# The order in which the moving operand's columns are read in seven input projections of a hybrid decoder layer

## The chip, the cores and the metric

The kernel runs on one core of one Trainium2 chip. The metric is the device time of one execution in microseconds (us); lower is better. Of the kernel before, two executions were timed, 2161.64 and 2170.17 us, with a median of 2165.9 us.

## What is computed

One decoder layer over 512 tokens of width 2048, in float32. One input projection is split by columns between gated linear attention (GLA, 4 heads) and differential softmax attention (4 heads). Their outputs pass through one output projection, and a gated MLP with a short causal convolution follows. The part that matters here is the first line of the token mixer:

```
proj = h @ w_in
offs = np.cumsum((0,) + IN_SPLITS)
gq, gk, gv, gg, ga, dq, dk, dv = [proj[..., int(offs[i]):int(offs[i + 1])]
                                  for i in range(len(IN_SPLITS))]
...
o_a = gla_chunked(gq..., gk..., gv..., log_a...)
o_b = diff_attention(dq..., dk..., dv, lam)
o = concatenate([rmsnorm(o_a) * gate, rmsnorm(o_b) * (1.0 - lambda_init)])
return o @ w_o
```

`h` is the normalised input (512 x 2048). The columns of `w_in` are 512 for gq, 512 for gk, 1024 for gv, 1024 for gg, 16 for ga, and 1024 each for dq, dk and dv.

## The kernel before, in words

**Number format.** Every large matrix product is done on numbers split in two. `ah` and `al` hold the high and low halves of the transposed activations, each as a tile of 128 partitions by (4 token groups, 16 slices of the model width, 128 tokens) of 4-byte fp32r numbers. A weight block of 128 x 1024 is loaded by one DMA (`load`, L100), and `granule` (L126) splits it: ScalarE copies the high half into the buffer `ring` (L135) and VectorE subtracts it to get the low half (L136). `ring` has three slots of a high and a low half. A product is then three matmuls, high by high, high by low, and low by high, all added into one PSUM bank of 128 x 512.

**Two forms of projection.** `proj_t` (L176) gives two 128-column pieces of the output with the tokens along the columns of the bank. The weight is the stationary operand, and the moving operand is `ah[:, t0:t1, kk, :]` or the same slice of `al`: four runs of 128 tokens. From one run to the next it is 16 x 128 elements of 4 bytes, 8192 bytes, and within a run the step is 4 bytes. One call has 4 granules, and each granule has 2 pieces x 4 slices x 3 = 24 matmuls, so it is 96 matmuls of 512 columns. `proj_n` (L194) gives 512 output columns for each of the four token groups, in four banks. Here `ah` and `al` are stationary and the weight is the moving operand: one run of 512 elements. One call has 8 granules of 4 token groups x 2 slices x 3 = 24 matmuls, so it is 192 matmuls of 512 columns. In both, the matmul writes its bank column by column in sequence.

**Evictions.** When a projection is complete, `emit` is called once per bank: two times in `proj_t`, four times in `proj_n`. For gq, gk, gv, dq, dk and dv it is one ScalarE copy of 128 x 512 from the bank to an SBUF tile (L311, L569, L571, L577, L583, L585). The gate (gg) has another form (L588).

**Order of the work.** After a first part whose order is written by hand (`first_half`, L219), the projections run in program order: gq and gk of heads 0 and 1, the second half of gv, gq and gk of heads 2 and 3, the first half of dv, dq and dk of differential head 0, of head 1, the second half of dv, dq and dk of heads 2 and 3, and then gg. After each granule, `step` (L84) takes one or two pieces from a list of small jobs (`fill`): forget gate, GLA heads, differential heads. Their small matmuls are thus placed between the projection's matmuls on TensorE's queue. A planner that estimates times sets the final order on each engine. The projections take their banks from a pool of four (`psm`), and the fill jobs from another pool of four. After the mixer come the output projection (L637 to L739) and the MLP, which together take most of the time and use the same `proj_t`, `mm_t`, `proj_n` and `mm_n` for a part of it.

Of the kernel before, what the change touches and what calls it, by code (L numbers as in the profile page):

```python
# [12 lines left out]
AF = mybir.ActivationFunctionType  # L13
# [4 lines left out]
P = 128  # L18
D = 2048
S = 512  # L20
NT = S // P
KT = D // P
EPS = 1e-6
GH, GDK, GDV, RANK = 4, 128, 256, 16
# [5 lines left out]
C_GQ, C_GK, C_GV, C_GG, C_GA, C_DQ, C_DK, C_DV = 0, 512, 1024, 2048, 3072, 3088, 4112, 5136  # L30
# [5 lines left out]
def hybrid_layer(ctx: ExitStack, tc: tile.TileContext, x, attn_pre_norm, w_in, w_alpha_up, b_alpha,  # L36
# [5 lines left out]
    w_in3 = w_in[0].rearrange("(k p) c -> p k c", p=P)  # L42
# [9 lines left out]
    act = nc.scalar.activation  # L52
# [3 lines left out]
    mm = nc.tensor.matmul  # L56
# [16 lines left out]
    ah = const.tile([P, NT, KT, P], F32R, name="ah")  # L73
    al = const.tile([P, NT, KT, P], F32R, name="al")
    wpool = ctx.enter_context(tc.tile_pool(name="w", bufs=3))

    def bank(pool=None):
        return (pool or psa).tile([P, 512], F32, name="bank", tag="bank")
# [5 lines left out]
    def step(n=None):  # L84
        pace[1] += pace[0]
        while pace[1] >= 1.0:
            pace[1] -= 1.0
            while fill:
                try:
                    next(fill[0])  # L90
                    break
                except StopIteration:
                    fill.pop(0)
# [6 lines left out]
    def load(src, a):  # L100
        raw = wpool.tile([P, GR], F32, name="raw", tag="raw", bufs=4)
        dma(raw.rearrange("p (a b) -> p a b", a=a), src)
        return raw
# [7 lines left out]
    def halves():  # L111
        slot[0] = (slot[0] + 1) % 3
        return [ring[:, GR * i + place_w[0]:GR * (i + 1) + place_w[0]] for i in (slot[0], slot[0] + 3)]
# [3 lines left out]
    def spare_halves(pool):  # L117
        if pool == "rt":
            return [rp.tile([P, GR], F32R, name=n, tag="rt", bufs=4) for n in ("xhi", "xlo")]
        if pool is True:  # L120
            if not kept:
                kept.extend(small_tile(n, F32R) for n in ("xhi", "xlo"))
            return kept
        return [pool.tile([P, GR], F32R, name=n, tag=n, bufs=4) for n in ("xhi", "xlo")]

    def granule(src, a, raw=None, spare=None, hl=None):  # L126
        if raw is None:
            raw = load(src, a)
        if hl is not None:
            hi, lo = hl[:, 0, :], hl[:, 1, :]  # L130
        elif spare:
            hi, lo = spare_halves(spare)
        else:
            hi, lo = halves()
        act(hi, raw, AF.Copy)  # L135
        tt(lo, raw, hi.bitcast(F32), ALU.subtract)  # L136
        r = "p (a b) -> p a b"
        return hi.rearrange(r, a=a), lo.rearrange(r, a=a)
# [21 lines left out]
    def bcast_row(tile_ap, row):  # L160
        dma(tile_ap, row.partition_broadcast(P))

    def mm_t(banks, g, w, t0, t1):
        for n in range(2):
            for k in range(4):
                kk = 4 * g + k
                wh = w[0][:, k, n * P:(n + 1) * P]
                wl = w[1][:, k, n * P:(n + 1) * P]
                o = banks[n][:, t0 * P:t1 * P].rearrange("p (t c) -> p t c", c=P)
                st, sp = kk == 0, kk == KT - 1  # L170
                mm(o, wh, ah[:, t0:t1, kk, :], start=st, stop=False)  # L171
                mm(o, wh, al[:, t0:t1, kk, :], start=False, stop=False)  # L172
                mm(o, wl, ah[:, t0:t1, kk, :], start=False, stop=sp)  # L173


    def proj_t(w3, col, emit):  # L176
        banks = [bank(psm) for _ in range(2)]
        for g in range(KT // 4):
            mm_t(banks, g, granule(w3[:, 4 * g:4 * g + 4, col:col + 256], 4), 0, NT)
            if g == KT // 4 - 1:  # L180
                for n in range(2):
                    emit(n, banks[n])
            step()

    def mm_n(banks, t, g, w):
        for k in range(2):
            s = 2 * g + k
            st, sp = s == 0, s == KT - 1
            mm(banks[t], ah[:, t, s, :], w[0][:, k, :], start=st, stop=False)  # L189
            mm(banks[t], ah[:, t, s, :], w[1][:, k, :], start=False, stop=False)  # L190
            mm(banks[t], al[:, t, s, :], w[0][:, k, :], start=False, stop=sp)  # L191


    def proj_n(w3, col, emit, order=tuple(range(KT)), first=0, banks=None):  # L194
        if banks is None:
            banks = [bank(psm) for _ in range(NT)]
        for g in range(first, KT // 2):
            w = granule(w3[:, order[2 * g]:order[2 * g] + 2, col:col + 512], 2)
            for t in range(NT):
                mm_n(banks, t, g, w)  # L200
                if g == KT // 2 - 1:
                    emit(t, banks[t])
            step()

    mixer = ExitStack()
# [3 lines left out]
    def big8(name):  # L209
        return mx.tile([P, 2048], F32, name=name, tag="big8", bufs=6)  # L210

    def qk_tile(name):
        return mx.tile([P, S], F32, name=name, tag="qk", bufs=6)
# [5 lines left out]
    def first_half(c):  # L219
# [37 lines left out]
        def prods(t, *gs):  # L257
            for g in gs:
                mm_n(banks, t, g, w[g])
# [46 lines left out]
    with tc.manual_schedule(engines=IN_ORDER):  # L306
        banks = first_half(0)
    gv = [big8("gv").rearrange("p (t e) -> p t e", t=NT) for _ in range(2)]

    def gv_out(c):  # L310
        return lambda t, b: act(gv[c][:, t, :], b, AF.Copy)  # L311

    proj_n(w_in3, C_GV, gv_out(0), first=4, banks=banks)


# [250 lines left out]

    def gla_qk(hp):
        q = [qk_tile("gq") for _ in range(2)]
        proj_t(w_in3, C_GQ + 256 * hp, lambda n, b: act(q[n], b, AF.Copy, scale=GDK ** -0.5))  # L569
        k = [qk_tile("gk") for _ in range(2)]  # L570
        proj_t(w_in3, C_GK + 256 * hp, lambda n, b: act(k[n], b, AF.Copy))  # L571
        for i in range(2):
            fill.append(gla_head(2 * hp + i, q[i], k[i]))

    def diff_v(g):
        dv = big8("dv").rearrange("p (t e) -> p t e", t=NT)
        proj_n(w_in3, C_DV + 512 * g, lambda t, b: act(dv[:, t, :], b, AF.Copy))  # L577
        dst = big8("dst").rearrange("p (j s) -> p j s", j=4)
        return dv, dst

    def diff_qk(h, dv, dst):
        q = [qk_tile("dq") for _ in range(2)]
        proj_t(w_in3, C_DQ + 256 * h, lambda n, b: act(q[n], b, AF.Copy))  # L583
        k = [qk_tile("dk") for _ in range(2)]
        proj_t(w_in3, C_DK + 256 * h, lambda n, b: act(k[n], b, AF.Copy))  # L585
        fill.append(diff_head(h, q, k, dv, dst))

    def gate(c, t, b):  # L588
# [4 lines left out]

    fill.append(forget_gate())
    gla_qk(0)
    pace[0] = 1.7
    proj_n(w_in3, C_GV + 512, gv_out(1))
    gla_qk(1)
    dsts = []
    for g in range(2):  # L600
        dv, dst = diff_v(g)
        dsts.append(dst)
        diff_qk(2 * g, dv, dst)
        pace[0] = 1.0
        diff_qk(2 * g + 1, dv, dst)
# [3 lines left out]
    for g in range(2):  # L609
        for j in range(4):  # L610
            s = 4 * g + j
# [29 lines left out]
    def to_ffn():  # L641
# [6 lines left out]
        def prods(t, *gs):  # L648
            for g in gs:
                mm_n(banks, t, g, w[g])  # L650
# [60 lines left out]
        ba = [bank(psm) for _ in range(2)]  # L711
        bb = [bank(psm) for _ in range(2)]
        mm_t(ba, 0, wa[0], 0, 2)
        residual(3)
        turn(2, 0, 1, 2, 3)
        square(3)
        weights_f(wa, 0, 3, wp)
        mm_t(ba, 1, wa[1], 0, 2)
        mm_t(ba, 2, wa[2], 0, 2)
        scale(3)  # L720
# [364 lines left out]
    for i, u in enumerate(downs):  # L1085
        nxt = downs[i + 1] if i + 1 < len(downs) else None
        nc_ = (i + 1) // 2
        first = i % 2 == 0
# [23 lines left out]
        else:  # L1112
            for j in range(2):
                for half, c, op in ((1, 0, ALU.add), (1, 1, ALU.subtract), (0, 1, ALU.subtract)):
                    dst = acc[2 * half + j].rearrange("p (b c x) -> p b c x", b=2, c=2)[:, :, c, :]
# [125 lines left out]
```

## Time and profile before

| | |
|---|---|
| timed executions | 2161.64 and 2170.17 us, median 2165.9 us |
| span of the profiled execution, first to last instruction | 2150.8 us |
| time of the profiled execution itself | not given beside its span; the median is 15.1 us above the span |
| TensorE busy (PE) | 2112.4 us, 98% of the span |
| TensorE weight loads (PEld) | 1875.4 us, 87% |
| VectorE busy (DVE) | 1414.6 us, 66% |
| ScalarE busy (ACT) | 898.3 us, 42% |
| DMA | 303.83 MB, mean 141 GB/s |

How to read it: the busy time of TensorE is the union of its matmuls, each of which lasts from its start to its modelled end. Matmuls are pipelined, so one starts before the one ahead of it has ended. What a matmul costs the engine is therefore the distance from its start to the next one's start, which the timeline gives, and not its duration in the list of groups. In the list of groups, a row is: line, engine, operation, the tile written and the tiles read, the shape, the count, then the busy time in us, the mean duration of one in ns, and the idle time of the engine before it.

### The profile page before, as it was taken

How to read it: one execution, taken by the hardware profiler on the slowest of the kernel's cores; microseconds unless marked ns; L12 is line 12 of the kernel's file. 1: busy time of each engine (PE TensorE's matmuls, PEld its weight loads, DVE VectorE, ACT ScalarE, POOL GpSimd, SP SyncE). 2: the span in 40 equal slices, each digit the busy share in tenths (PEclk: the TensorE clock that was granted, in tenths of full speed). 3: DMA queues.
4: the chain of work that ended last, by engine and by line, in shares of the span. 5: the costliest groups of instructions: out<-in, count | busy, mean ns of one | idle time of the engine just before them, and what ended most of it. 6: DMA issues, size and time to landing. Idle time of an engine off the chain costs nothing.

```text
span 2150.8 us, 31861 instructions
## 1 busy us (share of the span) xinstructions
PE 2112.4 (98%) x13009; PEld 1875.4 (87%) x13009; DVE 1414.6 (66%) x1725; ACT 898.3 (42%) x1162; POOL 199.2 (9%) x242
## 2 busy tenths in 40 slices
PE   7999999999999999999999999999999899999998
PEld 6878888888888889999999999999999778787786
DVE  5345554443444237688777786777778777888887
ACT  4233332333343224344544553544454554443433
POOL 1000000000000001011111111111110111110100
PEclk9999999999999999999999999999999999999999
DMA  6322222223224335455776757667577777676653
GB/s 214 99 75 79 79 69 79 79 79 88 78 80 169 95 128 186 128 119 136 172 172 149 175 139 189 149 157 191 129 172 177 203 229 182 171 195 170 158 167 145
DMA packets 218471, 303.83 MB, mean 141 GB/s; under 512 B 11776, under 2 KB 155572, under 8 KB 216404
## 3 DMA queue, kind: packets, MB, share of 16 engines
q1 hardware_dynamic: 165204, 238.87, 33.4%
q0 software_dynamic: 53120, 62.92, 19.1%
q8 instruction: 102, 1.67, 0.3%
q14 instruction: 45, 0.37, 0.1%
HBM read 273.97 MB, written 27.79 MB: 140 GB/s over the span
## 4 chain that ended last, share of the span: by engine, by line
PE 46%; issue 45%; POOL 4%; DVE 3%; DMA 2%; ACT 1%; POOLq 0%; SPq 0%; DVEq 0%; ACTq 0%
PE bank L189 7%; PE bank L190 7%; PE bank L191 7%; PE bank L173 5%; PE bank L171 5%; PE bank L172 5%; POOL rt L873 2%; PE bank L926 2%; PE bank L925 2%; PE bank L924 2%; POOL raw L873 2%; PE bank L439 1%; PE bank L507 1%; PE bank L538 1%; DVE ring L136 1%
## 5 line engine op out<-in xcount | busy, mean ns | idle before, releaser
L136 DVE TENSOR_TENSOR ring<-raw,ring 128x1024 fp32r<-128x1024 f32 x305 | 371.6, 1221 | 353.8 <-ACT ring L135 344.1
L135 ACT ACTIVATE ring<-raw 128x1024 fp32r<-128x1024 f32 x305 | 323.1, 1060 | 596.6 <-PE bank L191 157.3
L926 PE MATMUL bank<-ah,ring 128*128 128x256 f32 x1280 | 353.7, 276 | 0.8 <-DVE ring L136 0.8
L924 PE MATMUL bank<-ah,ring 128*128 128x256 f32 x1280 | 353.5, 276 | 0.0
L925 PE MATMUL bank<-al,ring 128*128 128x256 f32 x1280 | 353.4, 276 | 0.0
L136 DVE TENSOR_TENSOR ring<-rt,ring 128x1024 fp32r<-128x1024 f32 x221 | 269.0, 1220 | 89.8 <-ACT ring L135 87.9
L135 ACT ACTIVATE ring<-rt 128x1024 fp32r<-128x1024 f32 x221 | 233.1, 1060 | 223.5 <-PE bank L925 146.1
L926 PEld LDWEIGHTS bank<-ah,ring 128*128 128x128 f32 x1280 | 240.3, 188 | 1.2 <-DVE ring L136 1.2
L925 PEld LDWEIGHTS bank<-al,ring 128*128 128x128 f32 x1280 | 240.4, 188 | 0.1
L924 PEld LDWEIGHTS bank<-ah,ring 128*128 128x128 f32 x1280 | 240.3, 188 | 0.1
L189 PE MATMUL bank<-ring,ah 128*128 128x512 f32 x600 | 236.9, 398 | 0.8 <-ACT ah L148 0.8
L190 PE MATMUL bank<-ring,ah 128*128 128x512 f32 x600 | 235.8, 394 | 0.0
L191 PE MATMUL bank<-ring,al 128*128 128x512 f32 x600 | 235.0, 394 | 0.0
L171 PE MATMUL bank<-ah,ring 128*128 128x512 f32 (+1 forms) x512 | 196.2, 383 | 0.0
L173 PE MATMUL bank<-ah,ring 128*128 128x512 f32 (+1 forms) x512 | 194.7, 380 | 0.0
L172 PE MATMUL bank<-al,ring 128*128 128x512 f32 (+1 forms) x512 | 194.5, 380 | 0.0
L1022 PE MATMUL bank<-ring,ah 128*128 128x512 f32 x424 | 166.7, 393 | 7.3 <-DVE ring L136 7.2
L1023 PE MATMUL bank<-ring,al 128*128 128x512 f32 x424 | 165.8, 391 | 0.0
L1021 PE MATMUL bank<-ring,ah 128*128 128x512 f32 x424 | 158.8, 393 | 3.2 <-ACT ring L135 2.4
L191 PEld LDWEIGHTS bank<-ring,al 128*128 128x128 f32 x600 | 113.2, 189 | 24.3 <-DVE al L149 0.3
L189 PEld LDWEIGHTS bank<-ring,ah 128*128 128x128 f32 x600 | 113.1, 189 | 24.2 <-ACT ah L148 1.2
L190 PEld LDWEIGHTS bank<-ring,ah 128*128 128x128 f32 x600 | 113.3, 189 | 23.7 <-DVE ring L136 0.5
(260 smaller groups left out, 4063.6 us busy)
## 6 DMA issues: line engine op xcount, KB each, us to landing
raw<-in_w_in_dram SPq DMA_DIRECT2D x96, 512.0 KB, 3.7
raw<-in_w_ffn_in_dram SPq DMA_DIRECT2D x96, 512.0 KB, 5.1
raw<-in_w_ffn_out_dram SPq DMA_DIRECT2D x48, 512.0 KB, 7.3
rt<-in_w_ffn_in_dram SPq DMA_DIRECT2D x40, 512.0 KB, 6.6
rt<-in_w_ffn_in_dram POOLq DMA_DIRECT2D x40, 512.0 KB, 6.2
raw<-in_w_ffn_in_dram POOLq DMA_DIRECT2D x40, 512.0 KB, 6.8
raw<-in_w_o_dram SPq DMA_DIRECT2D x32, 512.0 KB, 3.7
rt<-in_w_ffn_out_dram SPq DMA_DIRECT2D x20, 512.0 KB, 8.1
```

The source lines that it names most:

```text
L135: act(hi, raw, AF.Copy)
L136: tt(lo, raw, hi.bitcast(F32), ALU.subtract)
L171: mm(o, wh, ah[:, t0:t1, kk, :], start=st, stop=False)
L172: mm(o, wh, al[:, t0:t1, kk, :], start=False, stop=False)
L173: mm(o, wl, ah[:, t0:t1, kk, :], start=False, stop=sp)
L189: mm(banks[t], ah[:, t, s, :], w[0][:, k, :], start=st, stop=False)
L190: mm(banks[t], ah[:, t, s, :], w[1][:, k, :], start=False, stop=False)
L191: mm(banks[t], al[:, t, s, :], w[0][:, k, :], start=False, stop=sp)
L924: mm(o, wh, sh[:, :, kk, :], start=start and kk == 0 and n == 0, stop=False, **NOW)
L925: mm(o, wh, sl[:, :, kk, :], start=False, stop=False, **NOW)
L926: mm(o, wl, sh[:, :, kk, :], start=False, stop=kk == HK - 1, **NOW)
L1022: mm(b[j], sh[:, o:o + P], w[1][:, q, :], start=False, stop=False, **NOW)
```

## The change

Seven of the input projections read the columns of the moving operand in another order. Bank columns are still written in sequence, so the result lies in the bank in the walked order, and the eviction writes its destination in that order, which puts every column back in its place. Two counters give each call of `proj_t` and of `proj_n` on `w_in` its walk; the calls after the list's end, the first call of `proj_n`, the first call of `proj_t`, and all calls on other weights keep the order of before.

The walks by projection, with `c` a column within a token group and `t` the token group:

| name here | projection | order of the moving operand's columns |
|---|---|---|
| T1 | gk, heads 0 and 1 | the four token groups innermost: each column lies 8192 bytes from the one before, and after four of them the next is 4 bytes further on |
| T2 | gq, heads 2 and 3 | in each token group every second column, then the others: step 8 bytes |
| T3 | gk, heads 2 and 3 | runs of 64 neighbouring columns, going through the token groups |
| T4 | dq, head 0 | runs of 16 neighbouring columns, going through the token groups |
| N1 | gv, second half | every sixteenth column: step 64 bytes |
| N2 | dv, first half | every second column, then the others: step 8 bytes |
| N3 | dv, second half | runs of 16 neighbouring columns, taken in turn from the two halves |

The core of the diff:

```diff
-    def mm_t(banks, g, w, t0, t1):
+    WALKS = {"t": [("p t c -> p t c", {}), ("p t c -> p c t", {}), ("p t (c b) -> p t b c", dict(b=2)),
+                   ("p t (b c) -> p b t c", dict(b=2)), ("p t (b c) -> p b t c", dict(b=8))],
+             "n": [("p c -> p c", {}), ("p (a b) -> p b a", dict(a=32)), ("p (b a) -> p a b", dict(a=2)),
+                   ("p (a b c) -> p b a c", dict(a=2, c=16))]}
+    calls = {"t": 0, "n": 0}
+
+    def next_walk(kind):
+        i = calls[kind]
+        calls[kind] += 1
+        return i if i < len(WALKS[kind]) else 0
+
+    def walk(kind, i, ap):
+        how, sizes = WALKS[kind][i]
+        return ap.rearrange(how, **sizes)
+
+    def as_walked(kind, i, b, like):
+        names = WALKS[kind][i][0].split("-> p ")[1]
+        dims = dict(zip(names.split(), walk(kind, i, like).shape[1:]))
+        first = names.split()[0]
+        dims.pop(first)
+        return b.rearrange(f"p ({names}) -> p {names}", **dims)
+
+    def mm_t(banks, g, w, t0, t1, i=0):
...
-                mm(o, wh, ah[:, t0:t1, kk, :], start=st, stop=False)
-                mm(o, wh, al[:, t0:t1, kk, :], start=False, stop=False)
-                mm(o, wl, ah[:, t0:t1, kk, :], start=False, stop=sp)
+                xh, xl = (walk("t", i, v[:, t0:t1, kk, :]) for v in (ah, al))
+                if i:
+                    o = as_walked("t", i, banks[n], ah[:, t0:t1, kk, :])
+                mm(o, wh, xh, start=st, stop=False)
+                mm(o, wh, xl, start=False, stop=False)
+                mm(o, wl, xh, start=False, stop=sp)
...
     def proj_t(w3, col, emit):
         banks = [bank(psm) for _ in range(2)]
+        i = next_walk("t") if w3 is w_in3 else 0
...
-    def mm_n(banks, t, g, w):
+    def mm_n(banks, t, g, w, i=0):
...
-            mm(banks[t], ah[:, t, s, :], w[0][:, k, :], start=st, stop=False)
-            mm(banks[t], ah[:, t, s, :], w[1][:, k, :], start=False, stop=False)
-            mm(banks[t], al[:, t, s, :], w[0][:, k, :], start=False, stop=sp)
+            wh, wl = (walk("n", i, v[:, k, :]) for v in w)
+            o = as_walked("n", i, banks[t], w[0][:, k, :]) if i else banks[t]
+            mm(o, ah[:, t, s, :], wh, start=st, stop=False)
+            mm(o, ah[:, t, s, :], wl, start=False, stop=False)
+            mm(o, al[:, t, s, :], wh, start=False, stop=sp)
...
+    def put_n(dst, b, i):
+        act(walk("n", i, dst), as_walked("n", i, b, dst), AF.Copy)
+
+    def put_t(dst, b, i, **kw):
+        d = dst.rearrange("p (t c) -> p t c", c=P)
+        act(walk("t", i, d), as_walked("t", i, b, d), AF.Copy, **kw)
+
     def gv_out(c):
-        return lambda t, b: act(gv[c][:, t, :], b, AF.Copy)
+        return lambda t, b, i=0: put_n(gv[c][:, t, :], b, i)
...
-        proj_t(w_in3, C_GK + 256 * hp, lambda n, b: act(k[n], b, AF.Copy))
+        proj_t(w_in3, C_GK + 256 * hp, lambda n, b, i=0: put_t(k[n], b, i))
```

The evictions of gq, dv, dq and dk are changed in the same way as that of gk.

More of the change, by code (lines that the diff above doesn't have):

```diff
@@ L170, in mm_t @@
                 st, sp = kk == 0, kk == KT - 1
-                mm(o, wh, ah[:, t0:t1, kk, :], start=st, stop=False)
-                mm(o, wh, al[:, t0:t1, kk, :], start=False, stop=False)
-                mm(o, wl, ah[:, t0:t1, kk, :], start=False, stop=sp)
+                xh, xl = (walk("t", i, v[:, t0:t1, kk, :]) for v in (ah, al))
[4 more added lines that the diff above has]
+                mm(o, wl, xh, start=False, stop=sp)
     def proj_t(w3, col, emit):
         banks = [bank(psm) for _ in range(2)]
+        i = next_walk("t") if w3 is w_in3 else 0
         for g in range(KT // 4):
-            mm_t(banks, g, granule(w3[:, 4 * g:4 * g + 4, col:col + 256], 4), 0, NT)
+            mm_t(banks, g, granule(w3[:, 4 * g:4 * g + 4, col:col + 256], 4), 0, NT, i)
             if g == KT // 4 - 1:
                 for n in range(2):
-                    emit(n, banks[n])
+                    if i:
+                        emit(n, banks[n], i)
+                    else:
+                        emit(n, banks[n])
             step()
-    def mm_n(banks, t, g, w):
+    def mm_n(banks, t, g, w, i=0):
         for k in range(2):
@@ L196, in proj_n @@
             banks = [bank(psm) for _ in range(NT)]
+        i = next_walk("n") if w3 is w_in3 else 0
         for g in range(first, KT // 2):
@@ L199, in proj_n @@
             for t in range(NT):
-                mm_n(banks, t, g, w)
+                mm_n(banks, t, g, w, i)
                 if g == KT // 2 - 1:
-                    emit(t, banks[t])
+                    if i:
+                        emit(t, banks[t], i)
+                    else:
+                        emit(t, banks[t])
             step()
@@ L568, in gla_qk @@
         q = [qk_tile("gq") for _ in range(2)]
-        proj_t(w_in3, C_GQ + 256 * hp, lambda n, b: act(q[n], b, AF.Copy, scale=GDK ** -0.5))
+        proj_t(w_in3, C_GQ + 256 * hp, lambda n, b, i=0: put_t(q[n], b, i, scale=GDK ** -0.5))
         k = [qk_tile("gk") for _ in range(2)]
-        proj_t(w_in3, C_GK + 256 * hp, lambda n, b: act(k[n], b, AF.Copy))
+        proj_t(w_in3, C_GK + 256 * hp, lambda n, b, i=0: put_t(k[n], b, i))
         for i in range(2):
@@ L576, in diff_v @@
         dv = big8("dv").rearrange("p (t e) -> p t e", t=NT)
-        proj_n(w_in3, C_DV + 512 * g, lambda t, b: act(dv[:, t, :], b, AF.Copy))
+        proj_n(w_in3, C_DV + 512 * g, lambda t, b, i=0: put_n(dv[:, t, :], b, i))
         dst = big8("dst").rearrange("p (j s) -> p j s", j=4)
@@ L582, in diff_qk @@
         q = [qk_tile("dq") for _ in range(2)]
-        proj_t(w_in3, C_DQ + 256 * h, lambda n, b: act(q[n], b, AF.Copy))
+        proj_t(w_in3, C_DQ + 256 * h, lambda n, b, i=0: put_t(q[n], b, i))
         k = [qk_tile("dk") for _ in range(2)]
-        proj_t(w_in3, C_DK + 256 * h, lambda n, b: act(k[n], b, AF.Copy))
+        proj_t(w_in3, C_DK + 256 * h, lambda n, b, i=0: put_t(k[n], b, i))
         fill.append(diff_head(h, q, k, dv, dst))
```

## Prediction

> **What bounds the kernel now.** I read the page first, for the engine that is full and its clock, then the chain of work that ended last, then the busy time by stretch for the changed projections, and then the timeline of TensorE, since only the distance between two starts says what a matmul costs there.
>
> ```profile
> span 2150.8 us, 31861 instructions
> PE 2112.4 (98%) x13009; PEld 1875.4 (87%) x13009; DVE 1414.6 (66%) x1725; ACT 898.3 (42%) x1162; POOL 199.2 (9%) x242
> PEclk9999999999999999999999999999999999999999
> PE bank L189 7%; PE bank L190 7%; PE bank L191 7%; PE bank L173 5%; PE bank L171 5%; PE bank L172 5%; POOL rt L873 2%; PE bank L926 2%; PE bank L925 2%; PE bank L924 2%; POOL raw L873 2%; PE bank L439 1%; PE bank L507 1%; PE bank L538 1%; DVE ring L136 1%
> ```
>
> TensorE is busy for 98% of the span, at full clock in every slice, and the chain that sets the end runs over the lines that the change touches (L171 to L173, L189 to L191). The busy time in the stretches of six of the seven projections, in the order T1, N1, T2, T3, N2, T4 (N3 is the last row; its cuts are rough):
>
> ```profile
> core 0: us, PE busy (x) PEld busy (x) DVE busy (x) ACT busy (x) POOL busy (x), PEclk, DMA share, GB/s
> 93.49:115.25 21.76, 21.76 (x97) 18.02 (x96) 4.90 (x5) 5.33 (x7) 0.00 (x0) 1.00 0.32 97
> 115.25:172.90 57.65, 57.65 (x269) 45.76 (x268) 31.50 (x49) 22.92 (x28) 0.00 (x0) 1.00 0.24 69
> 172.90:201.50 28.60, 28.60 (x140) 24.06 (x140) 15.82 (x28) 9.68 (x16) 2.43 (x4) 1.00 0.28 83
> 201.50:230.10 28.60, 28.60 (x153) 24.58 (x151) 16.98 (x34) 9.62 (x16) 1.72 (x4) 1.00 0.26 74
> 230.10:286.00 55.90, 55.90 (x286) 47.57 (x285) 31.71 (x57) 17.88 (x31) 3.63 (x8) 1.00 0.26 76
> 286.00:314.40 28.40, 28.40 (x133) 23.75 (x133) 13.49 (x23) 9.74 (x18) 3.36 (x6) 1.00 0.26 75
> 394.00:448.00 54.00, 53.52 (x243) 43.17 (x242) 25.16 (x57) 19.89 (x46) 3.69 (x10) 1.00 0.27 76
> ```
>
> Column 2 (length) equals PE busy in six of seven rows: TensorE never waits there, while DVE and ACT are busy for at most 60% and 40%. So whatever a matmul takes longer goes into the time in full, and there is no idle time in these stretches to take it up.
>
> **What a column costs today.** The timeline of TensorE: start, duration, line, tiles and shape.
>
> ```profile
> 93.49 0.39 PE L171 MATMUL bank<-ah,ring 128*128 128x512 f32 x1
> 93.72 0.39 PE L172 MATMUL bank<-al,ring 128*128 128x512 f32 x1
> ...
> 113.21 0.39 PE L171 MATMUL bank<-ah,ring 128*128 128x512 f32 x1
> 113.44 0.39 PE L172 MATMUL bank<-al,ring 128*128 128x512 f32 x1
> 113.66 0.39 PE L173 MATMUL bank<-ah,ring 128*128 128x512 f32 x1
> 113.89 0.39 PE L189 MATMUL bank<-ring,ah 128*128 128x512 f32 x1
> ...
> 115.25 0.39 PE L189 MATMUL bank<-ring,ah 128*128 128x512 f32 x1
> ```
>
> From 93.49 to 113.21 there are 87 matmuls: 19.72 / 87 = 0.2267 us each, though each is drawn 0.39 us long. That is 0.443 ns per column. From 113.89 to 115.25 six matmuls of `proj_n` take 1.36 us, 0.2267 us again. The first kind reads four runs with jumps of 8192 bytes between them, the second one single run: three such jumps cost nothing that can be read here. With 256 columns the same holds:
>
> ```profile
> 1199.81 0.28 PE L924 MATMUL bank<-ah,ring 128*128 128x256 f32 x1
> ...
> 1202.41 0.28 PE L926 MATMUL bank<-s5h,ring 128*128 128x256 f32 x1
> ```
>
> 23 matmuls in 2.60 us are 0.113 us each, 0.442 ns per column. So the time goes by columns read and not by weight loads. The trace of before has no fp32r matmul with a step other than 4 bytes, so the cost of the other steps has to be bounded. Two other rates of moving columns on the same engine are to be seen, from the chain of waits (start, length, count):
>
> ```profile
> 137.48 1.72 PE bank L395 x4
> 212.68 0.84 PE bank L439 x8
> ```
>
> L395 is a matmul in plain float32 with 512 columns: 1.72 / 4 = 0.43 us, 0.84 ns per column, half the rate of above. L439 has 64 columns, 0.84 / 8 = 0.105 us, or 1.64 ns per column, the slowest rate here. The other side is bounded by the weight load that goes with each matmul, 189 ns:
>
> ```profile
> L189 PEld LDWEIGHTS bank<-ring,ah 128*128 128x128 f32 x600 | 113.1, 189 | 24.2 <-ACT ah L148 1.2
> ```
>
> **The change part by part.** The order of instructions on each of the five engines is the same before and after, entry by entry; only 20 evictions on ScalarE have another shape, and 4 x 96 + 3 x 192 = 960 matmuls another walk. No DMA, wait or instruction is added or moved.
>
> *Far steps, T1 and N1.* 96 + 192 = 288 matmuls, in which each column is 8192 or 64 bytes from the one before. The ends are a gain down to the weight load (0.189 - 0.227 = -0.038 us each, -10.9 us in all) and 1.64 ns per column (0.840 - 0.227 = +0.613 us each, +176.6 us). Zero lies between. I take the rate of L395, the row of the same engine with the same 512 columns, as that of a stream which delivers a column only every other time: 0.430 - 0.2267 = 0.2033 us. T1: 96 x 0.2033 = 19.5 us; N1: 192 x 0.2033 = 39.0 us; together 58.6 us, all on the path.
>
> *Step of 8 bytes, T2 and N2.* Again 288 matmuls. The ends are -10.9 us and, at the rate of L395, +58.6 us. The nearest rows that show such a step are on VectorE. In a GLA head, L427 writes 256 elements in seven levels; at the last one the step is 8 bytes, at the first the runs are 64 elements long:
>
> ```profile
> L427 DVE TENSOR_TENSOR d<-bcum x28: 399/418/447, 155.3 to 334.8; 128x256 f32<-128x256 f32 x28
> ```
>
> Least, median and most are 399, 418 and 447 ns, so an 8-byte step costs VectorE at most 7%. I take 0 and keep both ends.
>
> *Long runs, T3, T4 and N3.* 96 + 96 + 192 matmuls, with 7, 31 and 31 jumps instead of 3 or none. Three jumps of 8192 bytes cost under 1 ns by the rows above. At a third of a nanosecond each, 31 jumps are 10 ns and 288 matmuls 3 us. I take 0, with +3 us and, as above, no more than -0.038 x 384 = -14.6 us as ends.
>
> *The evictions.* 2 x 4 + 4 x 3 = 20 copies.
>
> ```profile
> L571 ACT ACTIVATE gk<-bank 128x512 f32<-128x512 f32 x4 | 2.4, 589 | 3.8 <-PE bank L173 3.8
> L135 ACT ACTIVATE ring<-raw 128x1024 fp32r<-128x1024 f32 x305 | 323.1, 1060 | 596.6 <-PE bank L191 157.3 <-PE bank L925 112.5 <-PE bank L172 101.8
> ```
>
> 512 more elements cost ScalarE 1060 - 589 = 471 ns, so if a far step halved its rate, an eviction would take 1060 ns instead of 589. For T1 and N1 these are 6 x 0.47 = 2.8 us, for all 20 of them 9.4 us; the lower end is 0, as nothing in a longer path makes a copy shorter. I take 0: ScalarE is idle for 60% or more of each stretch above. What hides it is the next granules' high halves, made one to two granules ahead, and the other banks of the pool: behind an eviction on ScalarE's queue stand the next L135 and the fill jobs' copies, and TensorE waits for these only when the two spare ring slots are used up. If that cover were gone, 2.8 us would show, 9.4 us at most.
>
> **The sum.** 58.6 + 0 + 0 + 0 = 58.6 us. On the profiled execution's span that is 2150.8 + 58.6 = 2209.4 us. Its own time is not given; the median of the two runs, 2165.9 us, lies 15.1 us above the span, and with the same 15.1 us the time is **2224.5 us**, 2.7% above the median.
>
> [...] What the trace shows is contiguous reads at 0.443 ns per column, and no others in this format. [...]
>
> **The rivals.**
>
> *Any step but 4 bytes halves the rate.* Then T2 and N2 pay as T1 and N1 do: 2165.9 + 2 x 58.6 = 2283.1 us. For it: the fast rate needs two columns in the time in which L395 takes one, which neighbours in pairs would give, and VectorE reads at about 1.6 ns per element (418 / 256), so its rows cannot show a loss at 0.44 ns. [...]
>
> *The cost goes with the memory fetched.* If one fetch brings four neighbours and the contiguous stream already uses it up, a far step costs up to the 1.64 ns of L439 and an 8-byte step 0.84 ns: 2165.9 + 176.6 + 58.6 = 2401.1 us; with the 8-byte step free it is 2342.5 us. For it: fp32r takes 0.227 us for 512 columns while half of L395's 0.430 is 0.215, as though the stream were already held back a little. Against it: L439's rate is that of short matmuls with a weight load each, no sign of a slow read.
>
> *Nothing is lost.* The walk is only another sequence of addresses, and the read keeps its rate as over the jumps of `proj_t`: 2165.9 us, not slower. It decides if the 288 far matmuls keep to 0.227 us. For it: the jumps of 8192 bytes are free. Against it: there are only three in 512 columns.
>
> *A gain.* If the 12 ns between 0.227 and 0.215 are lost to neighbouring reads colliding, another order could win them: 960 x 0.012 = 11.5 us, 2154 us. Even down to the weight load it is 960 x 0.038 = 36 us, 2130 us, still under 2%.
>
> **How the numbers follow.** The forecast has 0.42; any step halved 0.18; cost by fetch 0.18 (its two forms together); nothing lost 0.14; only one of T1 (2185.4 us) and N1 (2204.9 us) pays 0.06; a gain 0.02. The predicted time is that of the forecast, 2224.5 us, and its own range is 2210 to 2240 us (its evictions and jumps add at most 12.4 us; a penalty a quarter smaller takes off 14.6). The range that should hold the time 8 times in 10 goes from N1 alone to the far end, 2200 to 2405 us; left out are no loss, a gain and T1 alone, about 0.19. A measurement of this kernel can tell about 2%, 43 us, from no change. Slower by more: the first three, 0.78, and a hundredth from a penalty that is larger on one of the walks alone, so 0.79; within 2%: 0.20; faster: 0.01, as the weight load leaves no room for it.
>
> **What would show it.** In the timeline after, the distance between starts should be 0.43 us in gk of heads 0 and 1 and in the second half of gv, and 0.227 us in the other five. Their stretches should grow by 19.5 and 39.0 us, still with PE busy throughout, and all else shift by a constant. A distance of 0.43 us in T2 or N2 would make it the first rival, 0.8 us in T1 or N1 the second, 0.227 us everywhere the third. The evictions of gk and gv should show 0.59 to 1.06 us. TensorE idle inside a stretch, behind an eviction or L135, would prove my cover wrong.

## The result, and the profile after

The changed kernel takes 2275.1 us (two runs, 2259.3 and 2291.0 us) against 2165.9 us before. The ratio as estimated from the runs is 1.053, with a 95% interval of 1.043 to 1.063 (these two medians alone give 1.050; the ratios and intervals further down are such estimates too). The kernel is slower, by 109 us, where 58.6 us were forecast. The two executions lie 32 us apart, so the account below is read from the traces.

The page of the changed kernel: the span, the busy engines, and a matmul of each form (L220 is L189 of before, L196 is L171). The last fence has L189 as the page of before gives it.

```profile
span 2257.6 us, 31863 instructions
PE 2221.9 (98%) x13009; PEld 1887.1 (84%) x13009; DVE 1416.4 (63%) x1725; ACT 903.9 (40%) x1162; POOL 199.2 (9%) x242
L220 PE MATMUL bank<-ring,ah 128*128 128x512 f32 x600 | 267.2, 448 | 0.9 <-ACT ah L148 0.9
L196 PE MATMUL bank<-ah,ring 128*128 128x512 f32 (+1 forms) x512 | 205.8, 402 | 0.0
```

```profile
L189 PE MATMUL bank<-ring,ah 128*128 128x512 f32 x600 | 236.9, 398 | 0.8 <-ACT ah L148 0.8
```

The span grew by 106.8 us and TensorE's busy time by 109.5 us; the busy times of VectorE, ScalarE and GpSimd moved by 6 us at most. The mean duration of L220 went from 398 to 448 ns, but it mixes walked and plain projections, so the stretches have to be taken one by one. Below they are cut at the start of each projection's last eviction, in the order T1, N1, T2, T3, N2, T4, N3. First the kernel before, then the changed one; column 2 is the length, column 3 TensorE's busy time.

```profile
93.07:114.83 21.76, 21.76 (x98) 18.02 (x97) 4.90 (x4) 5.33 (x7) 0.00 (x0) 1.00 0.32 97
114.83:172.08 57.25, 57.25 (x264) 45.28 (x262) 31.80 (x49) 22.52 (x28) 0.00 (x0) 1.00 0.23 66
172.08:200.89 28.81, 28.81 (x146) 24.38 (x145) 15.21 (x27) 9.93 (x17) 2.43 (x4) 1.00 0.31 90
200.89:229.44 28.55, 28.55 (x152) 24.55 (x151) 16.98 (x33) 9.62 (x18) 1.72 (x4) 1.00 0.26 74
229.44:285.26 55.82, 55.82 (x283) 47.36 (x281) 32.32 (x58) 17.72 (x32) 3.63 (x8) 1.00 0.26 76
285.26:313.78 28.52, 28.52 (x137) 23.99 (x136) 13.00 (x22) 9.87 (x17) 3.36 (x6) 1.00 0.26 74
406.22:448.10 41.88, 41.88 (x194) 34.75 (x193) 18.98 (x43) 15.96 (x36) 2.22 (x6) 1.00 0.30 85
```

```profile
92.68:119.79 27.11, 27.11 (x97) 18.16 (x96) 4.90 (x4) 5.77 (x7) 0.00 (x0) 1.00 0.26 78
119.79:216.61 96.82, 96.82 (x266) 49.08 (x264) 32.46 (x49) 24.59 (x27) 0.00 (x0) 1.00 0.15 44
216.61:266.60 49.99, 49.99 (x145) 26.10 (x144) 15.50 (x27) 10.28 (x17) 2.38 (x4) 1.00 0.15 42
266.60:295.38 28.78, 28.78 (x153) 24.75 (x152) 16.87 (x33) 9.66 (x18) 1.72 (x4) 1.00 0.25 73
295.38:394.02 98.64, 98.64 (x283) 51.20 (x281) 32.39 (x58) 17.99 (x32) 3.63 (x8) 1.00 0.15 43
394.02:422.85 28.83, 28.83 (x137) 24.02 (x136) 13.01 (x22) 9.88 (x17) 3.37 (x6) 1.00 0.25 74
515.61:559.35 43.74, 43.74 (x194) 35.11 (x193) 19.09 (x43) 15.98 (x36) 2.21 (x6) 1.00 0.28 84
```

Row by row the differences are +5.4 (T1), +39.6 (N1), +21.2 (T2), +0.2 (T3), +42.8 (N2), +0.3 (T4) and +1.9 us (N3), 111.3 us in all. PE busy equals the length in every row, the clock stays at 1.00, and VectorE and ScalarE are busy for nearly the same time. So the loss is in the matmuls alone. The 4.5 us by which the sum exceeds the growth of the span were won back elsewhere, nearly all after the last of these projections, in code that the change does not touch.

The timeline of TensorE in the changed kernel shows what one matmul costs. The first pair of rows is from T1, the second from N1, the third from T2.

```profile
93.69 0.45 PE L197 MATMUL bank<-al,ring 128*128 128x512 f32 x1
...
112.95 0.45 PE L196 MATMUL bank<-ah,ring 128*128 128x512 f32 x1
...
161.30 0.62 PE L221 MATMUL bank<-ring,ah 128*128 128x512 f32 x1
...
181.24 0.62 PE L222 MATMUL bank<-ring,al 128*128 128x512 f32 x1
...
218.61 0.63 PE L197 MATMUL bank<-al,ring 128*128 128x512 f32 x1
...
228.58 0.63 PE L198 MATMUL bank<-ah,ring 128*128 128x512 f32 x1
```

There are 68 steps in the first pair, 19.26 / 68 = 0.283 us; 46 in the second, 19.94 / 46 = 0.433 us; 22 in the third, 9.97 / 22 = 0.453 us. The plain order has 0.227 us. An 8-byte step is thus the dearest of the three, twice the plain order, while columns that lie 8192 bytes apart cost only a quarter more.

ScalarE's evictions in the changed kernel, one each of T1, N1 and T2:

```profile
115.71 1.06 ACT L350 ACTIVATE gk<-bank 128x512 f32<-128x512 f32 x1 [2.63 <-PE bank L198]
208.81 1.03 ACT L346 ACTIVATE gv<-bank 128x512 f32<-128x512 f32 x1 [2.37 <-PE bank L222]
259.33 0.62 ACT L350 ACTIVATE gq<-bank 128x512 f32<-128x512 f32 x1 [5.26 <-PE bank L198]
```

A write with far steps takes ScalarE 1.03 to 1.12 us instead of 0.59 (T1's second eviction is the longest), one with 8-byte steps 0.62 to 0.63 us. ScalarE had been idle before each of those shown, and TensorE did not stop.

### The profile page after: what moved, and what is told of

It reads as the page before. It is cut to its first block, busy times and chain, and to the rows that moved or that the text cites. A ratio compares the mean times of both kernels' runs of the same rounds, so it can differ in the third digit from the quotient of the medians.

```text
span 2257.6 us, 31863 instructions
## 1 busy us (share of the span) xinstructions
PE 2221.9 (98%) x13009; PEld 1887.1 (84%) x13009; DVE 1416.4 (63%) x1725; ACT 903.9 (40%) x1162; POOL 199.2 (9%) x242
## 4 chain that ended last, share of the span: by engine, by line
PE 69%; issue 22%; DVE 3%; DMA 3%; POOL 2%; ACT 1%; POOLq 0%; SPq 0%; DVEq 0%; ACTq 0%
PE bank L220 7%; PE bank L221 7%; PE bank L222 7%; PE bank L968 5%; PE bank L967 5%; PE bank L966 5%; PE bank L198 5%; PE bank L196 5%; PE bank L197 5%; PE bank L1064 3%; PE bank L1065 3%; PE bank L1063 3%; PE bank L481 1%; DVE ring L136 1%; DMA rt<-in_w_ffn_in_dram 1%
## 5 line engine op out<-in xcount | busy, mean ns | idle before, releaser
L220 PE MATMUL bank<-ring,ah 128*128 128x512 f32 x600 | 267.2, 448 | 0.9 <-ACT ah L148 0.9
L221 PE MATMUL bank<-ring,ah 128*128 128x512 f32 x600 | 266.6, 445 | 0.0
L222 PE MATMUL bank<-ring,al 128*128 128x512 f32 x600 | 265.8, 445 | 0.0
L196 PE MATMUL bank<-ah,ring 128*128 128x512 f32 (+1 forms) x512 | 205.8, 402 | 0.0
L197 PE MATMUL bank<-al,ring 128*128 128x512 f32 (+1 forms) x512 | 204.5, 399 | 0.0
L198 PE MATMUL bank<-ah,ring 128*128 128x512 f32 (+1 forms) x512 | 204.5, 399 | 0.0
L1064 PE MATMUL bank<-ring,ah 128*128 128x512 f32 x424 | 167.1, 394 | 7.0 <-DVE ring L136 6.8
L1065 PE MATMUL bank<-ring,al 128*128 128x512 f32 x424 | 166.1, 392 | 0.0
L1063 PE MATMUL bank<-ring,ah 128*128 128x512 f32 x424 | 158.4, 392 | 2.4 <-ACT ring L135 2.4
L220 PEld LDWEIGHTS bank<-ring,ah 128*128 128x128 f32 x600 | 115.4, 193 | 46.7 <-issue 26.6
```

What stands on the lines that cost most here:

```text
L196: mm(o, wh, xh, start=st, stop=False)
L197: mm(o, wh, xl, start=False, stop=False)
L198: mm(o, wl, xh, start=False, stop=sp)
L220: mm(o, ah[:, t, s, :], wh, start=st, stop=False)
L221: mm(o, ah[:, t, s, :], wl, start=False, stop=False)
L222: mm(o, al[:, t, s, :], wh, start=False, stop=sp)
```

## The experiments

In what follows A, B, C are groups of four neighbouring columns (16 bytes) that follow each other, E and F are groups elsewhere, and A0 to A3 are the four columns of A.

**Do the costs add up, and are the 8-byte steps really the larger half?** `e1_no8` gives T2 and N2 the plain order back, `e2_only8` leaves only these two walked. The entries of the list of walks that differ, with the projections' names added:

```diff
 # e1_no8
-("p t (c b) -> p t b c", dict(b=2))      # T2
-("p (b a) -> p a b", dict(a=2))          # N2
+("p t c -> p t c", {})
+("p c -> p c", {})
 # e2_only8: the same two entries stay, T1, T3, T4, N1 and N3 become plain
```

> The two walks with a step of 8 bytes (T2 and N2) go back to the plain order, the other five stay. In the profile of the changed kernel the stretch of T2 grew by 21.2 us and that of N2 by 42.8 us. If the loss is TensorE's own reading of the columns, it goes with the walk: 64 us less than the changed kernel, so some 2207 to 2213 us, and about 45 us over the kernel before, most of it N1 (39.6 us). If the loss were a matter of the evictions or of what else shares the stretch, less than half of the 64 us would come back, and the starts in dv's first half would still lie more than 0.3 us apart.

> T2 and N2 alone are walked, all else is plain. If the walks' costs simply add up: 2166 + 64 = 2230 us, starts 0.453 us apart in T2 and N2 and 0.227 us elsewhere. A time under 2200 us would say that the far walks make the 8-byte walks dearer.

Measured: `e1_no8` 2203.7 us, 1.018 times the kernel before (interval 1.006 to 1.030); `e2_only8` 2236.2 us, 1.033 times (1.025 to 1.042). The two excesses make 1.051, the full change 1.053. So the costs add, as closely as these intervals can tell. That the 8-byte steps are the larger part is shown by the stretches above (64.0 us against about 47 us), as the two intervals overlap. The starts agree: in `e1_no8` T2 and N2 are back at 0.23 us while T1 and N1 keep 0.283 and 0.433 us, and in `e2_only8` T2 and N2 keep 0.454 to 0.456 us while T1 is back at 0.227 us.

**Which walks are dear?** Three theories: (A) two neighbours are read at once; (B) groups of four are fetched and a few stay open; (C) the memory spanned is gone through. `s1_steps` gives each of fifteen projections a walk of its own, `s2_lines` does so for twelve, and some walks come twice.

```diff
 # s1_steps, s2_lines: only the list of walks and the first index change, e.g.
+        ('p t (c b) -> p c t b', {'b': 2}),      # pairs, then the next token group
+        ('p (u t) c -> p u c t', {'u': 2}),      # two token groups in turn
+        ('p t (a b) -> p b a t', {'b': 16}),     # four in turn, then 64 bytes further on
+        ('p (x a b) -> p x b a', {'a': 4, 'b': 16}),   # four 64 bytes apart in turn, used up
-    calls = {"t": 0, "n": 0}
+    calls = {"t": 1, "n": 0}
```

> A survey: all twelve projections of the first form and three of the second get a walk of their own (all undone by the evictions), read by the distance between starts, not by the time. Steps of 8, 16, 32, 64, 128 and 256 bytes within a token group; pairs, fours and eights of neighbours with a hop to the next token group after each; two token groups in turn instead of four; in the second form steps of 16 and 128 bytes, and pairs 64 bytes apart. Theory A (two neighbours are read at once, a column whose neighbour is not next costs a double turn): every step from 8 bytes on 0.43 to 0.46 us, pairs, fours and eights 0.227 us whatever the hop; T1's 0.284 us stays unexplained. Theory B (groups of four neighbours are fetched and a few of them are kept, so that a column is cheap when its group was touched a few columns ago): 8 bytes 0.45, 16 bytes and more up to 0.9 us or, where the fetches can overlap, 0.43; all hops with four groups in turn at most 0.284, as each group is used up in turn, and two groups in turn like T1 or cheaper. Theory C (the memory between the first and the last column is gone through, up to a cap of two turns per column): 8 bytes and more all 0.43 to 0.45, and hops are free.

> A second survey, read in the same way. Four token groups in turn as in T1, but the next column of a group 8, 16, 64, 128 or 256 bytes further on instead of 4, so that nothing fetched is used a second time soon; and in the second form four columns 16, 64 or 512 bytes apart in turn, then their neighbours, so that what is fetched is used four times. Theory B: the first kind loses T1's advantage and goes to 0.43 us or more, the second kind gets it, 0.28 us, whatever the distance. Theory A: no difference by what comes after, every column out of order costs the same, 0.43 us in both kinds, and T1 is cheap for another reason, the 8192 bytes between its columns: then the first kind stays at 0.284 us. A third outcome, the first kind at 0.284 and the second at 0.43, says that the distance between successive columns decides and not the use made of a fetch.

From the timeline of `s1_steps`, pairs with a hop of 8192 bytes (72 matmuls from the first row to the second) and two token groups in turn (65 from the third to the fourth):

```profile
80.49 0.75 PE L214 MATMUL bank<-ah,ring 128*128 128x512 f32 x1
...
112.56 0.64 PE L214 MATMUL bank<-ah,ring 128*128 128x512 f32 x1
...
703.78 0.46 PE L214 MATMUL bank<-ah,ring 128*128 128x512 f32 x1
...
717.89 0.38 PE L213 MATMUL bank<-al,ring 128*128 128x512 f32 x1
```

32.07 / 72 = 0.445 us and 14.11 / 65 = 0.217 us. From `s2_lines`, four token groups in turn with the next column 64 bytes further on (72 matmuls):

```profile
81.91 0.69 PE L212 MATMUL bank<-ah,ring 128*128 128x512 f32 x1
...
117.83 0.67 PE L212 MATMUL bank<-ah,ring 128*128 128x512 f32 x1
```

35.92 / 72 = 0.499 us. All the walks of these two surveys, with the distance between starts where no small job stands between:

| walk | us per matmul of 512 columns |
|---|---|
| two places in turn, each used up (8192, 16384 or 256 bytes apart) | 0.217 |
| four places in turn, each used up (8192, 512, 128, 64 or 16 bytes apart) | 0.27 to 0.28 |
| four neighbours, hop of 8192 bytes / eight neighbours, same hop | 0.27 / 0.23 |
| four token groups in turn, 8 bytes further on | 0.33 |
| eight or sixteen places in turn, each used up (64 or 128 bytes apart) | 0.44 |
| steps of 8 / 16 / 32 bytes | 0.45 / 0.46 / 0.43 |
| pairs, hop of 8192 bytes / pairs 64 bytes apart | 0.445 / 0.43 |
| four token groups in turn, 16 / 64 / 128 / 256 bytes further on | 0.48 / 0.50 / 0.46 / 0.49 |

Theory A falls: pairs should be free and cost as much as single columns. Theory C falls: two places in turn should be dear and are faster than the plain order. Theory B foretold most of the second survey, cheap where a fetch is used up and dear where it is not (the four token groups with 8 bytes lie between, 0.33 us where it gave 0.43 or more), but it cannot explain why pairs from four places (0.445) cost more than single columns from the same four places (T1, 0.283).

**Two readers?** Theory D fits which walks of the surveys are cheap and which are dear: the even and the odd columns of a walk go to two readers in turn, each at half the rate, and each keeps up only if it reads the same group of four twice in a row. By it each reader gets A0 A2 B0 B2 or A1 A3 B1 B3 in the plain order (0.227 us), two in a row. With two places in turn (0.217 us) it gets four in a row. With an 8-byte step (0.453 us) it gets A0 B0 C0, one in a row; with pairs from four places (0.445 us) also one. In T1 it goes to and fro between two groups; D itself has no price for that, and its 0.28 to 0.34 us is taken from the rows of the surveys. `s3_halves` sets it against theory E, which is B with the cost by the number of fetches. The gate's two projections (gg) read half of each group in one matmul, from two slices of the model width, so that their products are not the reference's.

```diff
 # s3_halves, walks of the second form
+        ('p (x a b) -> p x b a', {'a': 2, 'b': 4}),        # A0 B0 A1 B1
+        ('p (x a b) -> p x b a', {'a': 2, 'b': 2}),        # A0 A2 A1 A3
+        ('p (a c b) -> p c a b', {'a': 2, 'b': 2}),        # A0 A1 E0 E1 A2 A3 E2 E3
+        ('p k (l w e) -> p w l e k', {'w': 2, 'e': 2}),    # gg 0: A0 E0 A1 E1 B0 F0 B1 F1
+        ('p k (l w e) -> p w l k e', {'w': 2, 'e': 2}),    # gg 1: A0 A1 E0 E1 B0 B1 F0 F1
```

> The two surveys left two theories. Theory D: the even and the odd columns of a walk are read by two readers in turn, each at half the rate, and each keeps up only if it reads the same group of four neighbours (16 bytes) twice in a row. Theory E: groups of four are fetched, a few of them stay open for some columns, and the cost goes with the number of fetches. Walks here, all read by the distance between starts, A, B and E being groups of four neighbours: gv's second half A0 E0 A1 E1 with the two groups side by side (D 0.217 us as with two token groups in turn, E 0.217 to 0.227); dv's first half A0 A2 A1 A3 (both 0.217 to 0.227); dv's second half pairs in turn from two halves 1024 bytes apart, A0 A1 E0 E1 A2 A3 E2 E3 (D 0.28 to 0.34 us, since each reader goes to and fro between two groups; E 0.217 to 0.227, as these are the same two groups as before). The gate projections carry the test: in them only two neighbours of each four are read in one matmul, from two slices of the model width, so that their products are not the reference's. First half of gg: A0 E0 A1 E1 B0 F0 B1 F1: each reader gets two in a row, but each group is fetched for two columns only. D: 0.217 to 0.227 us. E: 0.43 us, as with the 8-byte step, which also takes two columns of each four. Second half: A0 A1 E0 E1 B0 B1 F0 F1, the same columns with the readers' turns spoilt: both 0.43 us.

The timeline of `s3_halves`, three pairs of rows: dv's second half (37 matmuls), the first half of gg (32), the second half of gg (8).

```profile
439.01 0.57 PE L242 MATMUL bank<-ring,ah 128*128 128x512 f32 x1
...
451.22 0.51 PE L243 MATMUL bank<-ring,ah 128*128 128x512 f32 x1
...
576.76 0.48 PE L242 MATMUL bank<-ring,ah 128*128 128x512 f32 x1
...
584.11 0.39 PE L244 MATMUL bank<-ring,al 128*128 128x512 f32 x1
...
640.67 0.68 PE L242 MATMUL bank<-ring,ah 128*128 128x512 f32 x1
...
644.54 0.68 PE L244 MATMUL bank<-ring,al 128*128 128x512 f32 x1
```

12.21 / 37 = 0.330 us, 7.35 / 32 = 0.230 us, and 3.87 / 8 = 0.484 us. The last two read the same columns of their weight blocks and differ in their order alone; one is as fast as the plain order, the other takes more than twice as long. Both patterns are nested loops of 128, 2 and 2 columns, so the cost does not come from how finely the pattern is cut up. Theory E gave 0.43 for the first of them, and 0.217 to 0.227 for the pairs of dv, and falls. Theory D gave 0.217 to 0.227 (0.230 measured), 0.28 to 0.34 for the pairs (0.330), and 0.43 for the last (0.484, more than it says). A0 B0 A1 B1 took 0.216 us and A0 A2 A1 A3 0.230 us, in which each reader has two in a row as in the plain order.

What these distances show, for the walks tried here, is a rule for the order. Walks in which each column has a column of its own group of four two places before or after it take 0.216 to 0.27 us; all others take 0.27 to 0.50 us, and those among them that leave a group and are back in it within four columns lie at the lower end (0.27 to 0.33 us). Two readers in turn would give such a rule, but so would one reader whose work on a column leans on the column two places before, and no run here tells the two apart.

**What stays open in D.** Four neighbours with a hop give each reader two in a row and yet cost more than the plain order. (Where no small job stands between, they take 0.270 us in `s1_steps`, not the 0.282 us of the expectation.)

```diff
 # s4_hops: fours, in turn from two, four and sixteen regions of the 512 columns
+        ('p (a c b) -> p c a b', {'a': 2, 'b': 4}),
+        ('p (a c b) -> p c a b', {'a': 4, 'b': 4}),
+        ('p (a c b) -> p c a b', {'a': 16, 'b': 4}),
```

> What theory D leaves open: four neighbours and then a hop of 8192 bytes gave 0.282 us in the first survey, though each of the two readers gets two in a row from its group of four, for which the plain order's 0.227 to 0.230 us was due. Here fours with a hop of 1024 bytes (two regions in turn, gv's second half), of 512 bytes (four regions, dv's first half) and of 128 bytes (sixteen regions, dv's second half), and again of 8192 bytes (gk of heads 0 and 1, dk of head 2). If leaving a group for one that is not the next costs extra whatever the distance: about 0.28 us in all. If only the large hop, or the return to the same place in four regions, does it: 0.227 to 0.240 us in those with 1024 and 128 bytes. The time itself is not of interest.

Measured: 0.250 us with 1024 bytes, 0.272 with 512, 0.247 with 128, and 0.268 with 8192 bytes. That is neither of the two outcomes: a hop after four columns costs at each of these distances, by 0.02 to 0.045 us, and more with four regions than with two or sixteen. D says nothing of what a change of groups costs, nor why going to and fro between two groups costs 0.28 us where each is used four times (T1) and 0.33 us where it is used twice. The causes of these are not settled.

**A version that beats both.** `e3_two_in_turn` uses the fast walk in fifteen projections; `e4_two_in_turn_mlp` also in the MLP's products of 256 columns.

```diff
 # e3_two_in_turn
+        ('p (u t) c -> p u c t', {'u': 2}),      # all twelve projections of the first form
+        ('p (a b) -> p b a', {'a': 2}),          # three of the second
 # e4_two_in_turn_mlp, up_prods
-            o = b[:, 256 * n:256 * (n + 1)].rearrange("p (t c) -> p t c", c=P)
+            o = b[:, 256 * n:256 * (n + 1)].rearrange("p (c t) -> p c t", c=P)
...
+                xh, xl = (x[:, :, kk, :].rearrange("p t c -> p c t") for x in (sh, sl))
...
-            v = b.rearrange("p (n t) -> p n t", n=2)
+            v = b.rearrange("p (n c t) -> p n t c", n=2, t=2)
```

> A version that may beat both kernels: the walk that came out faster than the plain order in the first survey, two runs in turn (0.217 instead of 0.227 to 0.230 us), in all twelve projections of the first form (two token groups in turn) and in three of the second (the two halves of the 512 columns in turn), with evictions that put the columns back. In the survey such a projection was 1.1 us shorter than before, so 12 x 1.1 = 13 us, and 3 x 2.2 = 7 us for the second form: 20 us less than the kernel before, 0.9%. If the evictions, which take 1.06 us instead of 0.59 in such a walk, were on the path, their 36 x 0.47 = 17 us would take most of that back.

> The version above, and the same walk in the MLP's first products with 256 columns (two token groups in turn, 6720 matmuls of 0.1133 us). If it saves 4% there too, 6720 x 0.0047 = 32 us, together 52 us less than the kernel before, 2.4%. The evictions there are VectorE's and ScalarE's, and now read the bank with a step of 8 bytes and write with 4 bytes; 20 of VectorE's are split in two. VectorE is busy for about 80% of that stage, so if its reads of the bank slow down by half, it becomes the bound and the gain is lost.

Measured: `e3_two_in_turn` 2135.8 us, 0.989 times the kernel before (0.981 to 0.997); `e4_two_in_turn_mlp` 2122.3 us, 0.982 times (0.977 to 0.988). Both intervals lie wholly below 1, so both are faster than either kernel, than the one before by about 1 and 2%. That the second is faster than the first is not settled: the intervals overlap, though the longest of its six executions (2125.1 us) lies just under the shortest of the first's six (2126.1 us). The stretch from the end of gv's first half to the end of dk, first in the kernel before, then in `e3_two_in_turn`:

```profile
68.68:553.91 485.23, 484.75 (x2278) 399.35 (x2277) 228.01 (x424) 162.96 (x283) 27.49 (x58) 1.00 0.28 80
```

```profile
68.10:532.58 464.48, 463.87 (x2278) 401.72 (x2277) 229.73 (x423) 178.20 (x283) 27.77 (x59) 1.00 0.29 83
```

It is 20.8 us shorter, as expected (20), though ScalarE's evictions take it 15.2 us more: they are hidden. In the MLP the gain was mis-sized: in the timeline of `e4_two_in_turn_mlp`

```profile
1199.83 0.28 PE L984 MATMUL bank<-al,ring 128*128 128x256 f32 x1
...
1202.96 0.28 PE L985 MATMUL bank<-ah,ring 128*128 128x256 f32 x1
```

28 matmuls take 3.13 us, 0.1118 us each instead of 0.1130 to 0.1134, not the 0.1087 that 4% would give. Over 6720 matmuls that is about 11 us, not 32. What holds the matmuls of 256 columns at 0.112 us was not tried. No run here writes a bank out of sequence, which would spare the evictions their far steps.

## Why the prediction was right or wrong

**What bounds the kernel: right.** TensorE had no idle time in the stretches before and has none after (busy for the whole length in all seven rows of both tables); each longer matmul went into the stretches in full, 111.3 us in all.

**Far steps, T1 and N1: the place right, the size right for one of two.** N1's term was 39.0 us and measured 39.6, a half rate (0.433 us). The half rate was the author's estimate: no row of before shows a far step in this format, and 0.43 us was taken from L395, a matmul in another one; that it fits N1 so closely does not show that the two are slow for the same reason, and some of it is luck. T1's term was 19.5 us and measured 5.4: its columns lie far apart, but each group of four is used up within sixteen columns. The step's mistake was to price by the distance from one column to the next. The walks tried here divide by how soon a group of four is read again: 0.216 to 0.27 us where each column has one of its own group two places before or after it, 0.27 to 0.50 us elsewhere, and T1, back in a group after four columns, at the lower end of these. Why T1 then pays a quarter and not nothing is open. The pair came to 45.0 us instead of 58.6, and in this part the rival in which N1 alone pays was the nearest.

**Step of 8 bytes, T2 and N2: wrong, and this is the step that failed.** It was taken as 0 and measured 21.2 + 42.8 = 64.0 us, the larger part of the loss and a little over the upper end that was kept (58.6 us). The reason given was that an 8-byte step costs VectorE almost nothing. That row is of an engine that takes 1.6 ns per element (418 / 256); TensorE takes 0.44 ns per column, and a slow engine's row cannot bound a fast one's loss. The first rival said so against it, and its time, 2283.1 us, came nearest to the 2275.1 us measured, but that is in part luck, as by its own mechanism it is wrong as well: T1 has no step of 4 bytes and pays a quarter, not the half rate.

**Long runs: right.** 2.4 us for T3, T4 and N3 together, within the +3 us kept for them, nearly all of it in N3.

**The evictions: right.** 1.03 to 1.12 us with far steps, one of the six a little over the bound of 1.06, and nothing of it on the path.

**The other rivals.** Cost by the memory fetched, at up to 0.84 us, fell with the starts in T1 and N1 (0.283 and 0.433 us); in the form of theory E it fell with `s3_halves`. No loss and a gain fell for this change; but the remark that the plain order is already held back a little was right, since two places in turn win the 0.01 us; that neighbouring reads collide is not shown by it.

**Two reads in a group of four.** The 0.453 us of T2 against the 0.230 us of gg's first half in `s3_halves` shows that two columns of a group of four are enough in one order and not in another. T2 has two in succession in each group and runs at half the plain rate (0.453 against 0.227 us). Counted for every second column, as theory D does, two in a row agree with T2, with N1 (0.433 us), with the pairs of the surveys (0.43 to 0.445 us) and with the two halves of gg (0.230 and 0.484 us), but the count does not give T1's quarter (0.283 us) or the cost of the fours with a hop (0.247 to 0.272 us). What in TensorE would make it so was not shown.

The sum of the terms was 58.6 us and came to 111.3, with the errors of two terms of opposite sign (-13.6 and +64.0). The time lies outside the forecast's own range (2210 to 2240 us); the wider range, 2200 to 2405 us, held because the rivals' ends had been left in it. That the kernel would be slower was right, but of the terms that made it so only N1's held its size. The 15.1 us between median and span, which the sum took over, is mostly a difference between executions: in the changed kernel's profiled execution, time and span (2259.3 and 2257.6 us) lie 1.7 us apart.

## What to carry to other kernels

In this kernel, where TensorE is full and reads 4-byte fp32r columns at 0.44 ns each, the order of the moving operand's columns was worth a factor of two (0.216 to 0.50 us for 512 columns). Where it is the same, try walks in which every second column, taken by itself, stays in the same group of four columns (16 bytes) for at least two reads in a row: they took 0.216 to 0.27 us here, all others 0.27 to 0.50 us. Two contiguous runs in turn were among the fastest, 4 to 5% faster than one run of 512 columns (0.216 to 0.217 us against 0.227), and the eviction that puts the columns back was hidden here because ScalarE had idle time (busy for 178.20 of 464.48 us in `e3_two_in_turn`). And do not bound the cost of an access on a fast engine (0.44 ns per column on TensorE) by the row of a slow one (1.6 ns per element on VectorE).

## What the hardware showed that was not expected

- The plain order is not the fastest: 0.227 us for 512 contiguous columns, 0.216 to 0.217 us for two runs in turn, whether they lie 16, 256, 1024, 8192 or 16384 bytes apart.
- An 8-byte step (0.453 us) is dearer than a 64-byte step (0.433 us), and 8192 bytes between all neighbours of a walk can cost as little as a quarter (0.283 us).
- The same 512 columns read as A0 E0 A1 E1 or as A0 A1 E0 E1, with the rest of each group left out, take 0.230 or 0.484 us. That TensorE has two readers in turn is argued from such distances and not shown; no profile shows them.
- ScalarE writes 512 elements with steps of 16, 64 or 512 bytes in 1.03 to 1.12 us instead of 0.59 (1.03 us with 64 bytes and 1.06 and 1.12 us with 512 bytes in the changed kernel, 1.11 us with two places 16 bytes apart in turn in `s3_halves`), and with 8-byte steps in 0.62 to 0.63 us.
